# Closing stages of a streaming-encoder layer: the last expert pairs, the overflow branch and the second norm rearranged

## The chip, the cores and the metric

The kernel runs on one core of a Trainium2 chip. Times are device microseconds of that core. The kernel before takes 1161.49 us (median of 3 runs, 1161.32 to 1161.60).

## The reference

One layer, 256 tokens of 1024 values, float32. A trunk of three branches (attention, pooling, state space) ends in a first LayerNorm. Behind it stands a mixture of experts, 4 of 32 for each token, and a second LayerNorm:

```python
x = _layer_norm(DEEPNORM_ALPHA * x + mix, ln1_g[l], ln1_b[l])
ffn = _moe(x, w_router[l], b_router[l], w_up[l], b_up[l], w_down[l], b_down[l])
x = _layer_norm(DEEPNORM_ALPHA * x + ffn, ln2_g[l], ln2_b[l])
# an expert: hu = x @ w_up + b_up
#   act = min(hu_even, 7) * sigmoid(1.702 * min(hu_even, 7)) * (clip(hu_odd, -7, 7) + 1)
#   y = act @ w_down + b_down, weighted by the token's softmax gate and added to its row
```

An expert has 12 MB of weights, all 32 have 403 million bytes, and every one of them is read once.

## The kernel before, in words

*The ring.* `ring` holds 22 slots of 128 partitions x 8 KB. A weight chunk is 1 MB and fills one. `load_more` (L105) issues a transfer on SyncE for each free slot, in the order of use; `done` frees a slot behind the last product that reads it, and `release` gives it to whoever stands in `wants` (`keep`, `drop`) or back to the stream. The last two chunks come in four pieces each, alternately. The pool `con`, of constants, lies ahead of the ring in each partition; its last tile is `junk`, 4 bytes.

*Expert pairs.* The 32 experts go in `NP` = 16 pairs of 24 chunks. Each expert of a pair has 64 token slots; both share the 128 rows of the products, one on each half. `hot` makes a one-hot matrix of tokens and slots, `gather` (L958) collects the tokens' rows with it, `gates_T` (L974) makes the transposed, gate-weighted one. Then come four `up_chunk` (L1033: bias, then 8 steps of products for each expert, four chunks) and two `down_chunk` (L1041). In `products` (L1021) each chunk of work has two halves of four steps; at the start of the second half the deferred work in `pending` is issued. `swiglu`/`gate_units` (L997) is the activation: VectorE and ScalarE operations on the result of an up chunk, issued one chunk later, and two transposes back. `scatter` (L1015) adds a down chunk's result to the four accumulators `accs[t][n]` (token half t, column half n), which stay in PSUM through all pairs. The order on every engine is that of the program text (`manual_schedule`).

*The end before.* In the last pair, behind the second up chunk, five slots are taken from the ring; `row_loads` loads the four norm vectors and GpSimd broadcasts them. Behind the fourth up chunk `residual` (L1073) makes alpha * (x1 * g1 + b1) with three VectorE operations for each token half, and `add_residual` (L1080) adds it to `accs` with the identity on TensorE, in the middle of the first down chunk. Both scatters of the last pair are issued directly behind their down chunks, the first one followed by the statistics of the left columns. `overflow` (L1086) handles experts with more than 64 tokens: every engine loads the largest count into a register and branches; in these runs the branch is not entered. It stands behind the last scatter. The closing norm (L1181 to L1223) has four quarters `finish(t, n)`: (0,0) on ScalarE and GpSimd, (1,0) on TensorE with diagonal matrices, (0,1) and (1,1) on VectorE.

Of the kernel before, what the change touches and what calls it, by code (L numbers as in the profile page):

```python
# [17 lines left out]
S = 256  # L18
# [45 lines left out]
def hybrid_layer(ctx: ExitStack, tc: tile.TileContext, wt, wm, pa, pb, pc, xin, bu, lnp, b_down, out):  # L64
# [17 lines left out]
    def place(f, dt=F32):  # L82
        return ring.tile([128, 2048], dt, tag=f"w{f}", name=f"w{f}")
# [21 lines left out]
    def load_more():  # L105
        while free and state["next"] < n_chunks:
            k = state["next"]
            if k < n_chunks - 2:
                sp.dma_start(out=slot(), in_=chunk_src(k))
            elif len(free) < 2:  # L110
                break
            else:
                pair = [(slot(), chunk_src(k + i)) for i in range(2)]
                for q in range(4):
                    qs = slice(512 * q, 512 * q + 512)
                    for t, src in pair:
                        sp.dma_start(out=t[:, qs], in_=src[:, qs])

# [23 lines left out]
    ones32 = con.tile([128, 32], F32)  # L142
    epst = con.tile([128, 2], F32)
    hpi = con.tile([128, 1], F32)
    junk = con.tile([128, 1], F32)


    ph1 = ExitStack()
# [806 lines left out]

    l1 = c_("ln1")

    def gather(oh):  # L958
        xg = mw.tile([128, 8, 128], F32, tag="xg", name="xg", bufs=1)
# [12 lines left out]
        return xg  # L972

    def gates_T(oh, g):  # L974
# [4 lines left out]
        gT = mwr.tile([128, S], F32, tag="gT", name="gT")  # L979
        dve.tensor_copy(gT, pt)  # L980
        return gT

# [58 lines left out]
    def down_chunk(p, n, at):  # L1041
        py = ph.tile([128, 512], F32, tag="hu", name="py")
        products(py, N_TRUNK + 24 * p + 16 + 4 * n, at, True)
        y = mwr.tile([128, 512], F32, tag="y", name="y")
        act.activation(out=y, in_=py, func=ACTF.Copy)  # L1045
        return y

    accs = [[pacc.tile([128, 512], F32, tag=f"acc{t}{n}", name=f"acc{t}{n}") for n in range(2)] for t in range(2)]
# [15 lines left out]
    rs2 = late.tile([128, 2, 2], F32)  # L1064


    def row_loads():
        for i in range(4):
            pool.dma_start(out=row[32 * i:32 * i + 1, 0], in_=lnp[0, i:i + 1])
        for i in range(4):  # L1070
            pool.partition_broadcast(lns[i // 2][:, i % 2], row[32 * i:32 * i + 1, 0])

    def residual():  # L1073
        g, b = lns[0][:, 0], lns[0][:, 1]
        for t in range(2):
            TT(base[:, t], x1[:, t], g, op=ALU.mult)
            TT(base[:, t], base[:, t], b, op=ALU.add)
            TS(base[:, t], base[:, t], ALPHA, None, op0=ALU.mult)

    def add_residual():  # L1080
        for t in range(2):
            for n in range(2):
                pe.matmul(accs[t][n], ident, base[:, t, n * 512:(n + 1) * 512], start=False, stop=True, skip_group_check=True)


    def overflow():  # L1086
        top = nc.values_load(cmaxi, min_val=0, max_val=S)
        cnt = [0]

        def wload(e, c):  # L1090
            w = place(free[cnt[0] % 4])
            cnt[0] += 1
            sp.dma_start(out=w, in_=wm[bass.ds(e, 1), c].rearrange("o p c -> (o p) c"))
            return w.rearrange("p (k c) -> p k c", k=4)

        with tc.If(top > SLOT):
            with tc.For_i(0, NE, 1) as e:
# [5 lines left out]
                for base in range(SLOT, S, 128):  # L1103
# [6 lines left out]
                    xg, gT = gather(oh), gates_T(oh, gh)  # L1110
                    at = mw.tile([128, 8, 128], F32, tag="at", name="at")
# [8 lines left out]
                    for n in range(2):  # L1120
# [5 lines left out]
                        y = mwr.tile([128, 512], F32, tag="y", name="y")  # L1126
                        act.activation(out=y, in_=py, func=ACTF.Copy)
                        scatter(gT, y, n)
            stats(0, 0)
            stats(0, 1)  # L1130
            stats(1, 0)
            TT(z2[:, 1, 0:512], accs[1][0], lns[1][:, 0, 0:512], op=ALU.mult)

    def stats(t, n):
        dve.bn_stats(out=st2[:, t, n], in_=accs[t][n])  # L1135

    gT = None
    for p in range(NP):
        ahead = slice(2 * p + 2, 2 * p + 4)
        at = mw.tile([128, 8, 128], F32, tag="at", name="at")  # L1140
        prev = None
        for n in range(4):
            hu = up_chunk(p, n, xg)
            if (p, n) == (NP - 1, 1):

                row, base, z2, *lns = (place(free.pop(0)).rearrange("p (t d) -> p t d", t=2) for _ in range(5))
                row_loads()
            if prev is not None:
                swiglu(*prev)
            if n == 2:  # L1150
                gT = gates_T(oh, gate[:, :, 2 * p:2 * p + 2])
            if n == 3 and p + 1 < NP:
                oh = hot(val[:, :, ahead])
            prev = (hu, at, n)

        pending.append(gate_units(*prev))
        if p + 1 == NP:
            residual()
            pending.append(add_residual)
        else:  # L1160
            nxt = gather(oh)
        y = down_chunk(p, 0, at)
        if p + 1 == NP:
            act.activation(out=junk, in_=epst[:, 0:1], func=ACTF.Sqrt)
            scatter(gT, y, 0)
            stats(0, 0)
            stats(1, 0)
            TT(z2[:, 1, 0:512], accs[1][0], lns[1][:, 0, 0:512], op=ALU.mult)
        else:
            pending.append(lambda gT=gT, y=y, p=p: scatter(gT, y, 0, p == 0))  # L1170
        y = down_chunk(p, 1, at)
        if p + 1 == NP:
            scatter(gT, y, 1)
        else:
            pending.append(lambda gT=gT, y=y, p=p: scatter(gT, y, 1, p == 0))
            if p == NP // 2:
                down_bias()
            xg = nxt


    ln2 = lns[1]  # L1181
    o3 = out.rearrange("(t p) d -> t p d", p=128)
    stats(0, 1)
    pz2 = ph.tile([128, 512], F32, tag="g", name="pz2")
    overflow()
    pe.matmul(pz2, ident, ln2[:, 1, 0:512], start=True, stop=True, skip_group_check=True)
    def scale(t):
# [3 lines left out]
    def finish(t, n):  # L1191
        ns = slice(n * 512, (n + 1) * 512)
        z, acc = z2[:, t, ns], accs[t][n]
        if (t, n) == (0, 0):
            act.activation(out=z, in_=acc, func=ACTF.Identity, scale=rs2[:, t, 0:1], bias=rs2[:, t, 1:2])
            pool.tensor_tensor(z, z, ln2[:, 0, ns], op=ALU.mult)
            pool.tensor_tensor(z, z, ln2[:, 1, ns], op=ALU.add)
        elif (t, n) == (1, 0):

            sc = late.tile([128, 2, 128], F32, name="sc")  # L1200
            for i in range(2):
                TS(sc[:, i], ident, rs2[:, t, i:i + 1], None, op0=ALU.mult)  # L1202
            pe.matmul(pz2, sc[:, 0], z, start=False, stop=False, skip_group_check=True)  # L1203
            pe.matmul(pz2, sc[:, 1], ln2[:, 0, ns], start=False, stop=True, skip_group_check=True)  # L1204
            act.activation(out=z, in_=pz2, func=ACTF.Copy)  # L1205
        else:
            STT(z, acc, mv2[:, t, 0:1], ln2[:, 0, ns], op0=ALU.subtract, op1=ALU.mult)
            STT(z, z, rs2[:, t, 0:1], ln2[:, 1, ns], op0=ALU.mult, op1=ALU.add)
        if (t, n) != (0, 0):
            (act if n == 0 else sp).dma_start(out=o3[t][:, ns], in_=z)  # L1210

    for t in range(2):
        if t:
            stats(1, 1)
        dve.bn_aggr(out=mv2[:, t], in_=st2[:, t])  # L1215
        act.activation(out=rs2[:, t, 0:1], in_=mv2[:, t, 1:2], func=ACTF.Sqrt, bias=epst[:, 0:1])  # L1216
    scale(0)
    finish(0, 0)
    scale(1)
    finish(1, 0)  # L1220
    finish(0, 1)
    sp.dma_start(out=o3[0][:, 0:512], in_=z2[:, 0, 0:512])
    finish(1, 1)  # L1223
    ps3.close()


# [117 lines left out]
```

## Time and profile before

| | |
|---|---|
| median of 3 runs | 1161.49 us |
| the profiled execution, its own time | 1161.53 us |
| its span | 1159.8 us |
| busy share of the span: TensorE, VectorE, ScalarE, GpSimd | 97%, 26%, 16%, 1% |
| read from HBM | 436 MB |

The busy share of TensorE counts from the start of a matmul to its modelled end, so it does not say that the engine works at its peak. The granted clock is 1.00 nearly everywhere (mean 0.997). In the views PE is TensorE, PEld its weight loads, DVE VectorE, ACT ScalarE, POOL GpSimd, SP SyncE; a q behind an engine's name means its sequencer. A float32 product is executed in two passes, so one matmul of the program has two rows in the trace.

### The profile page before, as it was taken

The page shows a single profiled execution, that of the slowest core. Times are in us where ns is not written, and L with a number is a line of the kernel's source. Part 1 is how long each engine was busy: PE and PEld are TensorE (multiplying, and loading weights), DVE is VectorE, ACT ScalarE, POOL GpSimd, SP SyncE. Part 2 cuts the span into 40 slices and gives each one's busy share as a digit, 9 for nine tenths or more (in the row PEclk, how much of TensorE's full clock was granted, in tenths as well). Part 3 has the DMA queues.
Part 4 walks back from the last instruction along what each step waited for, and adds up shares of the span by engine and source line. Part 5 has one row for each costly group of instructions (what it writes and reads, how often), then busy time and mean ns, then how long its engine had stood idle before and what let it go on. Part 6 is the DMA issues. An engine that isn't in the chain of part 4 may idle for free. (4 is left out here: it accounts for less than half of the span.)

```text
span 1159.8 us, 13362 instructions
## 1 busy us (share of the span) xinstructions
PE 1130.4 (97%) x5535; PEld 527.4 (45%) x5535; DVE 300.9 (26%) x710; ACT 184.7 (16%) x389; POOL 13.5 (1%) x19
## 2 busy tenths in 40 slices
PE   9999999999999999999999999999999999999996
PEld 6888986643434343434343433343434344334332
DVE  4798622430202111111212121111111111111042
ACT  4555410310101010101010101010101010101002
POOL 0000000000000000000000000000000000000100
PEclk9999999999999999999999999999999999999999
DMA  9733685699999999999999999999999999999992
GB/s 368 306 110 137 243 358 212 253 423 421 420 421 421 421 421 421 421 421 420 421 422 420 421 421 420 414 422 420 422 421 420 422 420 421 421 421 420 420 412 87
DMA packets 63169, 438.05 MB, mean 378 GB/s; under 512 B 7136, under 2 KB 7648, under 8 KB 10752
## 3 DMA queue, kind: packets, MB, share of 16 engines
q1 hardware_dynamic: 62064, 435.46, 91.2%
q10 hardware_dynamic: 864, 1.54, 0.4%
q8 instruction: 45, 0.74, 0.3%
q0 software_dynamic: 176, 0.15, 0.0%
q14 instruction: 20, 0.16, 0.0%
HBM read 436.07 MB, written 1.05 MB: 377 GB/s over the span
## 5 line engine op out<-in xcount | busy, mean ns | idle before, releaser
L1028 PE MATMUL hu<-w,xg 128*64 128x512 f32 x2048 | 480.9, 596 | 14.2 <-DMA w<-in_wm_dram 14.2
L1028 PEld LDWEIGHTS hu<-w,xg 128*64 128x64 f32 x2048 | 166.0, 137 | 316.0 <-issue 262.1
L1028 PE MATMUL py<-w,at 128*64 128x512 f32 x1024 | 231.5, 597 | 0.0
L1000 DVE TENSOR_SCALAR s<-hu 128x256 f32<-128x256 f32 x64 | 27.0, 422 | 581.6 <-PE hu L1028 581.6
L1028 PEld LDWEIGHTS py<-w,at 128*64 128x64 f32 x1024 | 70.5, 136 | 136.0 <-issue 129.6
L1011 ACT ACTIVATE at<-pta 128x256 f32<-128x256 f32 x64 | 24.5, 383 | 422.9 <-PE pta L1010 422.9
L1037 PE MATMUL hu<-bup,pc_sb 128*64 128x512 f32 x256 | 68.3, 605 | 0.0
L1017 PE MATMUL acc<-y,gT 128*128 128x512 f32 x128 | 63.5, 618 | 1.5 <-ACT y L1045 1.5
L248 PE MATMUL pm<-w,w 128*128 128x256 f32 x208 | 60.6, 291 | 0.8 <-ACT vsb L641 0.8
L965 PE MATMUL pg<-oh,x 128*128 128x128 f32 x512 | 59.9, 275 | 0.0
L249 PE MATMUL pm<-w,w 128*128 128x256 f32 x208 | 58.8, 283 | 0.0
L250 PE MATMUL pm<-w,w 128*128 128x256 f32 x208 | 58.8, 282 | 0.0
L965 PEld LDWEIGHTS pg<-oh,x 128*128 128x128 f32 x512 | 58.4, 192 | 0.1
L1001 ACT ACTIVATE hu<-s 128x256 f32<-128x256 f32 x64 | 24.6, 385 | 168.3 <-DVE s L1000 168.3
L1045 ACT ACTIVATE y<-py 128x512 f32<-128x512 f32 x32 | 19.1, 597 | 190.9 <-PE py L1028 190.9
L234 DVE TENSOR_TENSOR w<-w,w 128x1024 fp32r<-128x1024 f32 x30 | 36.5, 1219 | 19.3 <-ACT w L233 19.1
L248 PEld LDWEIGHTS pm<-w,w 128*128 128x128 f32 x208 | 39.7, 191 | 3.8 <-issue 1.7
L1017 PEld LDWEIGHTS acc<-y,gT 128*128 128x128 f32 x128 | 21.7, 189 | 42.9 <-issue 39.7
L249 PEld LDWEIGHTS pm<-w,w 128*128 128x128 f32 x208 | 39.8, 191 | 0.1
L250 PEld LDWEIGHTS pm<-w,w 128*128 128x128 f32 x208 | 39.8, 191 | 0.0
L233 ACT ACTIVATE w<-w 128x1024 fp32r<-128x1024 f32 x30 | 31.6, 1057 | 35.3 <-PE pm L250 25.1
L408 PE MATMUL pm<-w,w 128*128 128x256 f32 x160 | 36.1, 383 | 1.1 <-DMA w<-in_wt_dram 1.1
(320 smaller groups left out, 681.8 us busy)
## 6 DMA issues: line engine op xcount, KB each, us to landing
w<-in_wm_dram SPq DMA_DIRECT2D x382, 1024.0 KB, 19.8
w<-in_wt_dram SPq DMA_DIRECT2D x26, 1024.0 KB, 7.9
w<-in_wm_dram SPq DMA_DIRECT2D x8, 256.0 KB, 11.7
w<-in_wt_dram SPq DMA_DIRECT2D x4, 256.0 KB, 5.6
w<-in_wt_dram ACTq DMA_DIRECT2D x4, 256.0 KB, 5.9
w<-in_wt_dram SPq DMA_DIRECT2D x2, 512.0 KB, 5.0
w<-in_xin_dram SPq DMA_DIRECT2D x1, 1024.0 KB, 7.7
w<-in_pb_dram SPq DMA_DIRECT2D x1, 896.0 KB, 8.5
```

The costliest lines, as they stand in the source:

```text
L233: act.activation(out=hi, in_=src, func=ACTF.Copy)
L234: TT(lo, src, hi.bitcast(F32), op=ALU.subtract)
L248: pe.matmul(out, whi, ahi, start=first, stop=False)
L249: pe.matmul(out, whi, alo, start=False, stop=False)
L250: pe.matmul(out, wlo, ahi, start=False, stop=last)
L408: pe.matmul(dst, w[:, k * 128:(k + 1) * 128], xt3[:, k], start=(k == 0), stop=(k == 7))
L965: pe.matmul(pg[:, b], x1[:, t, k * 128:(k + 1) * 128], oh[:, t], start=(t == 0), stop=(t == 1))
L1000: TS(xg, hu[:, 0:256], 7.0, None, op0=ALU.min)
L1001: act.activation(out=th, in_=xg, func=ACTF.Tanh, scale=0.851)
L1017: pe.matmul(accs[t][n], gT[:, t * 128:(t + 1) * 128], y, start=first, stop=True, skip_group_check=True)
L1028: pe.matmul(dst[64 * e:64 * e + 64], lhs[:, k, 64 * e:64 * e + 64], w[:, k % 4], start=first and k == 0, stop=(k == 7))
L1037: pe.matmul(hu[64 * e:64 * e + 64], ident[:, i:i + 1].to_broadcast([128, 64]), bup, start=True, stop=False)
```

## The change

The ring gets its base moved: `junk` becomes a column of a tile `scr` of 96 bytes. The last four chunks come in pieces, the first two of them in halves. Row loads and broadcasts go to pair NP-3 (the third from the end), where the four next slots released are kept; `residual` is issued there in two steps of two operations, and `add_residual` in that pair's first down chunk, behind which two slots go back. The counter is read into the registers in pair NP-4. In the last pair the activation of the second up chunk and `gates_T` are issued directly behind that chunk, then `overflow`, with weights in two free slots and its inputs in two others. The last down chunk's result is evicted in halves on ScalarE and VectorE. The left columns' scatter, statistics and products with the norm's scale are deferred into the last down chunk. The closing norm's left quarters go over TensorE (bias, diagonal matrices made by ScalarE), the right quarters and the very last step over VectorE; GpSimd has no part in it.

```diff
@@ load_more
-            if k < n_chunks - 2:
+            if k < n_chunks - 4:
                 sp.dma_start(out=slot(), in_=chunk_src(k))
             elif len(free) < 2:
                 break
             else:
                 pair = [(slot(), chunk_src(k + i)) for i in range(2)]
-                for q in range(4):
-                    qs = slice(512 * q, 512 * q + 512)
+                w = 1024 if k == n_chunks - 4 else 512
+                for q in range(0, 2048, w):
+                    qs = slice(q, q + w)
                     for t, src in pair:
                         sp.dma_start(out=t[:, qs], in_=src[:, qs])
@@ constants
-    junk = con.tile([128, 1], F32)
+    scr = con.tile([128, 24], F32)
+    junk = scr[:, 0:1]
@@ down_chunk
-        act.activation(out=y, in_=py, func=ACTF.Copy)
+        if (p, n) == (NP - 1, 1):
+            y = [y[:, 0:256], place(free[0])[:, 0:256]]
+            act.activation(out=y[0], in_=py[:, 0:256], func=ACTF.Copy)
+            dve.tensor_copy(y[1], py[:, 256:512])
+        else:
+            act.activation(out=y, in_=py, func=ACTF.Copy)
@@ residual
-    def residual():
-        g, b = lns[0][:, 0], lns[0][:, 1]
-        for t in range(2):
-            TT(base[:, t], x1[:, t], g, op=ALU.mult)
-            TT(base[:, t], base[:, t], b, op=ALU.add)
-            TS(base[:, t], base[:, t], ALPHA, None, op0=ALU.mult)
+    def residual(t):
+        base, l1r = rows_of("base"), rows_of("ln1")
+        STT(base[:, t], x1[:, t], ALPHA, l1r[:, 0], op0=ALU.mult, op1=ALU.mult)
+        STT(base[:, t], l1r[:, 1], ALPHA, base[:, t], op0=ALU.mult, op1=ALU.add)
@@ the loop over pairs
+        last = p + 1 == NP
...
+        if p == NP - 4:
+            top = nc.values_load(cmaxi, min_val=0, max_val=S)
+        if p == NP - 3:
+            for name in ("z2", "ln1", "ln2", "base"):
+                keep(name)
         for n in range(4):
             hu = up_chunk(p, n, xg)
-            if (p, n) == (NP - 1, 1):
-                row, base, z2, *lns = (place(free.pop(0)).rearrange("p (t d) -> p t d", t=2) for _ in range(5))
-                row_loads()
             if prev is not None:
                 swiglu(*prev)
-            if n == 2:
+            if p == NP - 3:
+                if n == 0:
+                    row_loads()
+                elif n > 1:
+                    residual(n - 2)
+            if n == (1 if last else 2):
                 gT = gates_T(oh, gate[:, :, 2 * p:2 * p + 2])
...
             prev = (hu, at, n)
+            if last and n == 1:
+                swiglu(*prev)
+                prev = None
+                overflow()
+                act.activation(out=junk, in_=epst[:, 0:1], func=ACTF.Tanh)
         pending.append(gate_units(*prev))
-        if p + 1 == NP:
-            residual()
+        if p == NP - 3:
             pending.append(add_residual)
...
         y = down_chunk(p, 0, at)
-        if p + 1 == NP:
+        if last:
             act.activation(out=junk, in_=epst[:, 0:1], func=ACTF.Sqrt)
-            scatter(gT, y, 0)
-            stats(0, 0)
-            stats(1, 0)
-            TT(z2[:, 1, 0:512], accs[1][0], lns[1][:, 0, 0:512], op=ALU.mult)
+            z2, ln2 = rows_of("z2"), rows_of("ln2")
+            def left_sums(y=y):
+                scatter(gT, y, 0)
+                for t in range(2):
+                    stats(t, 0)
+                    TT(z2[:, t, 0:512], accs[t][0], ln2[:, 0, 0:512], op=ALU.mult)
+            pending.append(left_sums)
...
         y = down_chunk(p, 1, at)
-        if p + 1 == NP:
-            scatter(gT, y, 1)
+        if last:
+            for t in range(2):
+                for h in range(2):
+                    pe.matmul(accs[t][1][:, h * 256:h * 256 + 256], gT[:, t * 128:(t + 1) * 128], y[h], start=False, stop=True, skip_group_check=True)
@@ closing norm (the four quarters finish(t, n) go; overflow() before them goes)
+    pz2 = [ph.tile([128, 512], F32, tag="g", name="pz2") for _ in range(2)]
+    for t in range(2):
+        pe.matmul(pz2[t], ident, ln2[:, 1, 0:512], start=True, stop=False, skip_group_check=True)
+    sc = late.tile([128, 2, 2, 128], F32, name="sc")
+    def moments(t):
+        stats(t, 1)
+        dve.bn_aggr(out=mv2[:, t], in_=st2[:, t])
+        act.activation(out=rs2[:, t, 0:1], in_=mv2[:, t, 1:2], func=ACTF.Sqrt, bias=epst[:, 0:1])
+    def scales(t):
         dve.reciprocal(rs2[:, t, 0:1], rs2[:, t, 0:1])
         STT(rs2[:, t, 1:2], mv2[:, t, 0:1], -1.0, rs2[:, t, 0:1], op0=ALU.mult, op1=ALU.mult)
+        for i in (1, 0) if t == 0 else (1,):
+            act.activation(out=sc[:, t, i], in_=ident, func=ACTF.Copy, scale=rs2[:, t, i:i + 1])
+    def left(t):
+        z = z2[:, t, 0:512]
+        pe.matmul(pz2[t], sc[:, t, 1], ln2[:, 0, 0:512], start=False, stop=(t == 1), skip_group_check=True)
+        if t == 0:
+            pe.matmul(pz2[t], sc[:, t, 0], z, start=False, stop=True, skip_group_check=True)
+            act.activation(out=z, in_=pz2[t], func=ACTF.Copy)
+            act.dma_start(out=o3[t][:, 0:512], in_=z)
+    def right(t):
+        z = z2[:, t, 512:1024]
+        STT(z, accs[t][1], mv2[:, t, 0:1], ln2[:, 0, 512:1024], op0=ALU.subtract, op1=ALU.mult)
+        STT(z, z, rs2[:, t, 0:1], ln2[:, 1, 512:1024], op0=ALU.mult, op1=ALU.add)
+        sp.dma_start(out=o3[t][:, 512:1024], in_=z)
+    moments(0)
+    moments(1)
+    scales(0)
+    scales(1)
+    left(0)
+    left(1)
+    right(0)
+    right(1)
+    z = z2[:, 1, 0:512]
+    STT(z, z, rs2[:, 1, 0:1], pz2[1], op0=ALU.mult, op1=ALU.add)
+    sp.dma_start(out=o3[1][:, 0:512], in_=z)
```

## Rows read from the trace of the kernel before

**Rows 1.** The page: its span, and GB/s in 40 slices of 29 us.

```profile
span 1159.8 us, 13362 instructions
...
GB/s 368 306 110 137 243 358 212 253 423 421 420 421 421 421 421 421 421 421 420 421 422 420 421 421 420 414 422 420 422 421 420 422 420 421 421 421 420 420 412 87
```

**Rows 2.** A window, stream's end: us, busy (count) of PE..POOL, clock, DMA share, GB/s.

```profile
1136.00:1137.00 1.00, 1.00 (x3) 0.38 (x2) 0.20 (x1) 0.99 (x2) 0.00 (x0) 1.00 0.25 92
```

**Rows 3.** Timeline of SyncE, last weight transfers: start us, us, line, operation, tile.

```profile
1129.35 0.33 SPq L117 DMA_DIRECT2D w<-in_wm_dram  x1
...
1131.82 0.33 SPq L117 DMA_DIRECT2D w<-in_wm_dram  x1
```

**Rows 4.** Timeline, last pair: start, us, line, operation, tiles, count [idle before <-releaser].

```profile
1097.18 3.65 PE L1028 MATMUL hu<-w,xg 128*64 128x512 f32 x14 [0.84 <-DMA w<-in_wm_dram]
...
1100.76 0.44 PE L1010 MATMUL pta<-pc_sb,s 128*128 128x128 f32 x2
...
1101.13 1.08 PE L1037 MATMUL hu<-bup,pc_sb 128*64 128x512 f32 x4
...
1126.26 1.98 PE L1083 MATMUL acc<-w,pc_sb 128*128 128x512 f32 x4 [0.34 <-DVE w L1078]
...
1129.38 1.98 PE L1083 MATMUL acc<-w,pc_sb 128*128 128x512 f32 x4 [1.14 <-DVE w L1078]
...
1137.56 7.09 PE L1028 MATMUL py<-w,at 128*64 128x512 f32 x32
...
1145.43 1.98 PE L1017 MATMUL acc<-y,gT 128*128 128x512 f32 x4 [0.78 <-ACT y L1045]
...
1149.94 1.10 PE L1186 MATMUL pz<-w,pc_sb 128*128 128x512 f32 x2 [2.53 <-PEq L1096]
...
1155.82 0.36 ACTq L1210 DMA_DIRECT2D out_dram<-w  x1
```

**Rows 5.** Groups by line, last 75 us: count | busy, mean ns | idle.

```profile
L1135 DVE BATCH_NORM_STATS2 st<-acc 128x6 f32<-128x512 f32 x4 | 2.8, 699 | 16.8 <-PE acc L1017 15.3 <-PEq L1096 1.5
...
L1207 DVE SCALAR_TENSOR_TENSOR w<-acc,mv,w 128x512 f32<-128x512 f32 x2 | 1.5, 742 | 0.0
...
L1045 ACT ACTIVATE y<-py 128x512 f32<-128x512 f32 x2 | 1.2, 597 | 16.3 <-PE py L1028 16.3
...
L980 DVE COPY gT<-ptw 128x256 f32<-128x256 f32 x1 | 0.4, 424 | 6.8 <-PE ptw L978 6.8
...
L1215 DVE BATCH_NORM_AGGREGATE mv<-st 128x2 f32<-128x12 f32 x2 | 0.4, 209 | 0.7 <-DVEq L1096 0.6
...
L1168 DVE TENSOR_TENSOR w<-acc,w 128x512 f32<-128x512 f32 x1 | 0.7, 674 | 0.0
```

**Rows 6.** The branch's line, on TensorE's sequencer: count, ns min/median/max, start us.

```profile
L1096 PEldq COMPARE_BRANCH  x1: 3489/3489/3489, 1146.0 to 1146.0; - x1
```

**Rows 7.** Windows of the tail, columns as in rows 2.

```profile
1151.00:1152.00 1.00, 0.46 (x2) 0.30 (x2) 0.97 (x5) 0.64 (x1) 0.00 (x0) 0.91 0.00 0
...
1152.00:1153.00 1.00, 1.00 (x2) 0.34 (x1) 0.89 (x2) 0.00 (x0) 0.87 (x1) 0.50 0.03 8
...
1155.00:1156.00 1.00, 0.15 (x1) 0.00 (x0) 0.61 (x1) 0.60 (x1) 0.06 (x1) 0.88 0.56 211
```

**Rows 8.** DMA queues: 400:600, 1153:1159.8 and 1136.9:1137.5 us; packets, MB, share of 16 engines.

```profile
q1 hardware_dynamic: 11542, 84.05, 101.1%
...
q1 hardware_dynamic: 432, 0.79, 31.0%
...
q14 instruction: 1, 0.01, 3.2%
```

**Rows 9.** DMA issues on the page: tiles, engine, count, KB each, us to landing.

```profile
w<-in_wm_dram SPq DMA_DIRECT2D x382, 1024.0 KB, 19.8
...
out_dram<-w SPq DMA_DIRECT2D x3, 256.0 KB, 2.1
...
out_dram<-w ACTq DMA_DIRECT2D x1, 256.0 KB, 2.7
```

More of the change, by code (lines that the diff above doesn't have):

```diff
@@ L956, in hybrid_layer, with gather @@
     l1 = c_("ln1")
-    def gather(oh):
-        xg = mw.tile([128, 8, 128], F32, tag="xg", name="xg", bufs=1)
+    def gather(oh, xg=None):
+        if xg is None:
+            xg = mw.tile([128, 8, 128], F32, tag="xg", name="xg", bufs=1)
         for g in range(2):
@@ L972, in gather, with gates_T @@
         return xg
-    def gates_T(oh, g):
+    def gates_T(oh, g, gT=None):
         TT(oh, oh, g[:, :, :, None].to_broadcast([128, 2, 2, SLOT]), op=ALU.mult)
@@ L978, in gates_T @@
             pe.transpose(pt[:, t * 128:(t + 1) * 128], oh[:, t], ident)
-        gT = mwr.tile([128, S], F32, tag="gT", name="gT")
+        if gT is None:
+            gT = mwr.tile([128, S], F32, tag="gT", name="gT")
         dve.tensor_copy(gT, pt)
@@ L1064, in hybrid_layer, with rows_of @@
     rs2 = late.tile([128, 2, 2], F32)
+    def rows_of(name):
+        return big[name][0].rearrange("p (t d) -> p t d", t=2)
     def row_loads():
+        row = rows_of("z2")
         for i in range(4):
@@ L1070, in row_loads @@
         for i in range(4):
-            pool.partition_broadcast(lns[i // 2][:, i % 2], row[32 * i:32 * i + 1, 0])
-    def residual():
-        g, b = lns[0][:, 0], lns[0][:, 1]
-        for t in range(2):
-            TT(base[:, t], x1[:, t], g, op=ALU.mult)
-            TT(base[:, t], base[:, t], b, op=ALU.add)
-            TS(base[:, t], base[:, t], ALPHA, None, op0=ALU.mult)
+            pool.partition_broadcast(rows_of(f"ln{i // 2 + 1}")[:, i % 2], row[32 * i:32 * i + 1, 0])
+    def residual(t):
+        base, l1r = rows_of("base"), rows_of("ln1")
+        STT(base[:, t], x1[:, t], ALPHA, l1r[:, 0], op0=ALU.mult, op1=ALU.mult)
+        STT(base[:, t], l1r[:, 1], ALPHA, base[:, t], op0=ALU.mult, op1=ALU.add)
     def add_residual():
+        base = rows_of("base")
         for t in range(2):
@@ L1083, in add_residual @@
                 pe.matmul(accs[t][n], ident, base[:, t, n * 512:(n + 1) * 512], start=False, stop=True, skip_group_check=True)
+        drop("base")
+        drop("ln1")
     def overflow():
-        top = nc.values_load(cmaxi, min_val=0, max_val=S)
+        assert state["next"] == n_chunks
         cnt = [0]
+        oxa = place(free[2]).rearrange("p (a k c) -> p a k c", a=2, k=8)
+        ogT = place(free[3])[:, 0:S]
         def wload(e, c):
-            w = place(free[cnt[0] % 4])
+            w = place(free[cnt[0] % 2])
             cnt[0] += 1
@@ L1109, in overflow @@
                     oh = hot(vh)
-                    xg, gT = gather(oh), gates_T(oh, gh)
-                    at = mw.tile([128, 8, 128], F32, tag="at", name="at")
+                    xg, gT, at = gather(oh, oxa[:, 0]), gates_T(oh, gh, ogT), oxa[:, 1]
                     for n in range(4):
@@ L1141, in hybrid_layer @@
         prev = None
+        if p == NP - 4:
[3 more added lines that the diff above has]
+                keep(name)
         for n in range(4):
             hu = up_chunk(p, n, xg)
-            if (p, n) == (NP - 1, 1):
-                row, base, z2, *lns = (place(free.pop(0)).rearrange("p (t d) -> p t d", t=2) for _ in range(5))
-                row_loads()
             if prev is not None:
                 swiglu(*prev)
-            if n == 2:
+            if p == NP - 3:
[4 more added lines that the diff above has]
+            if n == (1 if last else 2):
                 gT = gates_T(oh, gate[:, :, 2 * p:2 * p + 2])
-            if n == 3 and p + 1 < NP:
+            if n == 3 and not last:
                 oh = hot(val[:, :, ahead])
             prev = (hu, at, n)
+            if last and n == 1:
[3 more added lines that the diff above has]
+                act.activation(out=junk, in_=epst[:, 0:1], func=ACTF.Tanh)
         pending.append(gate_units(*prev))
-        if p + 1 == NP:
-            residual()
+        if p == NP - 3:
             pending.append(add_residual)
-        else:
+        if not last:
             nxt = gather(oh)
         y = down_chunk(p, 0, at)
-        if p + 1 == NP:
+        if last:
             act.activation(out=junk, in_=epst[:, 0:1], func=ACTF.Sqrt)
-            scatter(gT, y, 0)
-            stats(0, 0)
-            stats(1, 0)
-            TT(z2[:, 1, 0:512], accs[1][0], lns[1][:, 0, 0:512], op=ALU.mult)
+            z2, ln2 = rows_of("z2"), rows_of("ln2")
[5 more added lines that the diff above has]
+            pending.append(left_sums)
         else:
@@ L1178, in hybrid_layer @@
             xg = nxt
-    ln2 = lns[1]
     o3 = out.rearrange("(t p) d -> t p d", p=128)
[L1183 to L1187, printed above, removed]
+    pz2 = [ph.tile([128, 512], F32, tag="g", name="pz2") for _ in range(2)]
+    for t in range(2):
+        pe.matmul(pz2[t], ident, ln2[:, 1, 0:512], start=True, stop=False, skip_group_check=True)
+    sc = late.tile([128, 2, 2, 128], F32, name="sc")
@@ L1188, in scale @@
+    def moments(t):
[3 more added lines that the diff above has]
+    def scales(t):
         dve.reciprocal(rs2[:, t, 0:1], rs2[:, t, 0:1])
         STT(rs2[:, t, 1:2], mv2[:, t, 0:1], -1.0, rs2[:, t, 0:1], op0=ALU.mult, op1=ALU.mult)
[L1191 to L1223, printed above, removed]
+        for i in (1, 0) if t == 0 else (1,):
+            act.activation(out=sc[:, t, i], in_=ident, func=ACTF.Copy, scale=rs2[:, t, i:i + 1])
```

1 line of the change is left out of this document (removed).

## The prediction

> **What bounds the kernel now.** I read the slices of the span first, then windows of the middle and of the end, then SyncE's queue in order of time, then TensorE's timeline of the last expert pair. [rows 1] From about 230 us on the transfers run flat at 421 GB/s with the DMA engines busy all the time; TensorE is busy too, but it has slack, since each half of a chunk begins with a wait for a weight transfer (0.84 us before 1097.18 [rows 4]; the other halves of the pair are of this kind). So the weight stream sets the pace up to its last byte, and nothing before that is worth anything unless it makes a transfer faster. SyncE issues one transfer per landing, every 2.48 us [rows 3], the last at 1131.82; bytes move until about 1137 [rows 2]. The span ends at 1159.8. These 23 us behind the stream are what the change can reach, and in them two things are seen [rows 4]: TensorE stops for the residual (1126.26 to 1131.36, 1.14 us of it waiting for VectorE), so that the whole last down chunk starts only at 1137.56, when all its weights are there, and ends at 1144.65; then 15.15 us follow to the end (scatter, overflow branch, norm, stores).
>
> **The sum, made against the profiled run** (span 1159.8, time 1161.53, so 1.73 lie around the span; the median of the runs is 1161.49, practically the same).
>
> *Residual and row loads two pairs earlier.* Off the last pair go 8 passes of the identity (two groups of 1.98 us [rows 4]) and the wait between them, 5.1 us in all. In pair NP-3 the same 8 passes and four vector operations come back, now two per half of the rows instead of three. There TensorE has the slack seen above, some 1 us in each 10 us, and this pair and the next are 120 us long: I cost it at 0; without that cover it would be 3.9 us. Broadcasts on GpSimd and the row loads move along; the vector work behind them waits one chunk, and TensorE first needs VectorE's result a chunk later still. Four ring slots of 22 are held for one pair, then two: SyncE has 8 transfers out at a time (19.8 us from issue to landing at 2.48 us each) and its issue waits for a landing, not for a slot, so 0; if a slot were late, 2.48 us each.
>
> *The last four chunks in pieces.* The stream's end stays: the old last chunks in pieces of 256 KB kept the pace of 2.48 us per MB (1131.82 to about 1137 is 2 MB). TensorE may begin the first quarter of the last down chunk some 2.5 us before its half has landed. 0 by itself, bounds -0.5 and +0.5.
>
> *The overflow branch amid the last pair.* It leaves the tail, where TensorE idled 2.53 us for it (the wait before 1149.94 [rows 4]). On TensorE the branch itself took 3489 ns, on the other engines 45 to 72 ns [rows 6]. (The Trainium skill, "Runtime: NRT & Kernel Launch", Instruction fetch mechanics, says that a taken branch out of the fetched window has to fetch its target by DMA first; the row agrees. It speaks against the new place, where such a fetch meets the weight stream.) Behind the branch on TensorE now wait 2 up and 2 down chunks, and they are followed by everything else. Its arrival: the second up chunk ends where it does now, 1100.8; two pairs of transposes of some 0.35 us; then, because the second chunk's activation is no longer put behind the third chunk, TensorE waits for a chain of VectorE copy, four operations and ScalarE's tanh beside one of them, five of 0.42 us [rows 5] with gaps, 2.2 us; transposes again, 1104.1; the branch from 1103.75, 3.49, and 0.4 to the first load: 1107.65. What is queued: third and fourth up chunk, each 0.9 of bias (1.08 [rows 4] with some 0.2 of drain) and 7.0 (two halves, 3.58 from one to the next instruction), 15.8; first down chunk 7.16 and two transposes, 0.8; last down chunk 3.58, scatter of its neighbour 1.9, then 3.65: 32.9 in sum, 1140.55. All weights are there in time (the half of 1126.9 is awaited by nothing, the last quarters land by 1137). Two things are added. The engine has stood for 2.2 and 3.5 us; in the tail of before, after standing for 2.53 us, its granted clock fell to 0.50, the 1.2 GHz level, at about 1151.8 and was back at 1155.2 (means of 0.91, 0.50 and 0.88 [rows 7]), 3.4 us; I take one such stretch, in which 1.7 us of work is lost: **1142.2**. And the branch under load: bounds 0 (it hides nothing there) and 19.8 us (a fetch that stands behind the stream like a weight load); I take 0 extra, since the row of the branch itself is the nearest. The best case is set by the stream: the half landed at 1131.82 leaves 1.75, 1.9 and 3.65: 1139.2. The counter that the branch tests is now read in pair NP-4, by every engine: on SyncE behind seven transfers that are already out, on TensorE in the waits for weights, below 2.5 us (all that the read and the branch cost in the tail), so 0; the gate transposes move one chunk up and find their inputs ready, 0. ScalarE's table load behind the branch falls in the free time of two chunks. SyncE reaches the branch only after its last issue, waits there for all landings until about 1137.6, and holds up the output stores alone, which come later.
>
> *The tail, counted from TensorE's last down product T (now T is 1144.65, the tail 15.15).* Eviction in halves on ScalarE and VectorE, 0.13 and 0.42 [rows 5] instead of 0.13 and 0.60; scatter from T+0.6 in half-width pieces, same columns, 1.98 [rows 4], its first half done at T+1.6. Statistics 0.70, aggregate 0.21, twice, to T+3.5 on VectorE; the square root of the first lies beside them, that of the second ends at 3.9, and reciprocal and product of both at 4.2. TensorE meanwhile puts the bias into both banks, 4 passes of 0.43, which keep it going until 4.2; then ScalarE's diagonal matrices (128 columns each, below the 0.60 of 512 [rows 5]) and six passes, 2.6 us, to T+7.0. VectorE: four operations of 0.74 and 0.67 [rows 5] for the right halves, to T+7.1, and the last one, 0.74, which takes the bank just finished: T+7.9. Its store takes 2.1 us [rows 9] and the end of the span 1.3 more (before, ScalarE's store issued at 1155.82 [rows 4] lands 2.7 later [rows 9], at 1158.5), with 0.2 for the issue: **T+11.5**. So 15.15 becomes 11.5, of which 2.5 is the branch. If the clock is at the lower level there, six passes take twice the 2.6 us, and some more: T+14.2. The lower end is T+10.8.
>
> Span 1142.2 + 11.5 = 1153.7, time **1155.4**: 6.1 us below, 2.4 of it before T and 3.7 behind.
>
> *The ring at 1 KB multiples.* 64 bytes more ahead of it; before, every slot began 192 bytes past a multiple of 256. What a packet costs [rows 8]: the stream's packets took 101.1% of 16 engines for 200 us; 84.05 MB are 10260 of 8 KB, 315 ns each. The stores' 2 KB packets took 87.8 ns (31.0% of 16 x 6.8 us over the 384 that 0.79 MB are). So 8 KB cost 301 ns of bytes and some 14 of a fixed part, 4.4%. The gain lies between 0 and all of it over the 905 us of the flat stream, 40 us. I take 0: a packet of 8 KB of the instruction queue, which has nothing to do with the ring, takes 307 ns on an empty fabric (3.2% of 16 x 0.6 us), so the fixed part is there without the ring's offset.
>
> **The rivals.**
> 1. *Alignment counts.* If a packet that begins off a 256-byte line touches 33 lines instead of 32, each is 3.0% shorter afterwards: 905 us x 3.0% = 27 us, time **1128**. TensorE could follow (it waits in every half). For it: the fixed part is large enough. Against: the instruction packet. (The rule is that of the Trainium skill, "DMA: Bandwidth & Descriptors", How a descriptor splits into AXI transactions: a descriptor off a 256-byte boundary costs an extra transaction. No run here has an aligned ring, so nothing shows it yet.) Chance 0.14.
> 2. *The branch waits for the stream (slower).* Place: TensorE at 1103.75. Price: anything up to 19.8 us instead of 3.5. It decides from 9.6 us on, where the 6.1 us are gone; with the full price T is near 1158.5, the time **1172**. For it: the fetch goes through the same 16 engines. Against: instruction packets are fetched all through the stream, and TensorE shows no such gap [rows 4]. Chance 0.08.
> 3. *The gain is eaten (no change).* The branch costs 3 us more and the clock is low again in the tail: T 1145.2, tail 14.2, time **1161**; what is saved in one place is paid in another. Chance 0.09.
>
> **How the numbers follow.** Forecast 0.69: 1155.4, its own range 1151.7 (T 1139.2, tail 10.8) to 1159.3. The range to hold 8 in 10 reaches from 1146, which takes in a small effect of the alignment, to 1161; outside are rival 1 in full and rival 2. Within 0.2% is 2.3 us, about what this kernel's measurement can tell from no change. Faster 0.69 + 0.14 = 0.83, same 0.09, slower 0.08.
>
> **What would show it.** In the changed profile: transfers still at 421 GB/s in the middle (425 and more: rival 1); TensorE idle for 3.5 to 5 us around 1104 to 1108 at the branch (over 9: rival 2), and a clock of 0.50 soon after; the last down products ending near 1142 without waits for DMA but those of the pieces; no branch behind the scatter; the last store issued 8 us after T by SyncE, released by VectorE. I am wrong if the end of the stream itself moves, or if T is that of before.

## The result, and the profile after

| | before | after |
|---|---|---|
| median, runs side by side (4 each) | 1161.55 us | 1147.38 us |
| ratio | | 0.9877 (0.9860 to 0.9894) |
| profiled execution: time, span | 1161.53, 1159.8 | 1147.84, 1146.1 |
| last weight bytes | 1136.6 | 1126.3 |
| end of the last down product, T | 1144.65 | 1134.38 |
| T to the end of the span | 15.15 | 11.72 |

The change gains 14.2 us where 6.1 were forecast. In the span of the profiled runs 10.3 of 13.7 us are the stream's earlier end; T lies as far behind it as before, 8.0 us; and 3.4 are the tail's.

Six of the runs told of below, of kernels with slots at a multiple of 256 bytes, took 6 to 18 us more than their fellows; that is taken up behind the offsets.

The page of the changed kernel, against [rows 1]:

```profile
span 1146.1 us, 13388 instructions
...
GB/s 358 325 90 132 243 358 248 222 415 427 427 426 426 426 427 427 427 426 427 426 427 426 428 426 427 420 428 426 426 427 426 427 426 427 426 426 427 427 416 117
```

The flat stretch is at 427 GB/s, not 421. The row of its queue from 400 to 600 us (packets, MB, share of 16 engines), against [rows 8]:

```profile
q1 hardware_dynamic: 11693, 85.17, 100.9%
```

More bytes came in the same 200 us, with the engines as busy. In the records of the single packets the mean time of one of 8 KB between 300 and 1100 us went from 314.3 to 309.6 ns: before, 7% of them took 309 and nearly all others 311 to 321; after, 99.7% took 309. So the floor of 309 stayed, and what went is the spread above it.

TensorE's timeline in the last pair, against [rows 4]:

```profile
1089.32 0.44 PE L1015 MATMUL pta<-pc_sb,s 128*128 128x128 f32 x2
1089.59 0.38 PE L982 MATMUL ptw<-pc_sb,oh 128*128 128x128 f32 x2
1092.77 0.41 PE L1015 MATMUL pta<-pc_sb,s 128*128 128x128 f32 x2 [2.79 <-DVE s L1010]
1099.08 1.98 PE L1042 MATMUL hu<-bup,pc_sb 128*64 128x512 f32 x4 [5.90 <-PEq L1114]
...
1110.50 7.05 PE L1033 MATMUL hu<-w,xg 128*64 128x512 f32 x32
...
1121.80 7.09 PE L1033 MATMUL py<-w,at 128*64 128x512 f32 x32
1128.82 1.98 PE L1022 MATMUL acc<-y,gT 128*128 128x512 f32 x4
1130.73 3.65 PE L1033 MATMUL py<-w,at 128*64 128x512 f32 x16
```

The two waits are the chain of the activation (2.79) and the branch (5.90). Behind them no product waits for a weight: TensorE works off its lateness to the end. The branch's row on its sequencer, against [rows 6]:

```profile
L1114 PEldq COMPARE_BRANCH  x1: 5972/5972/5972, 1092.8 to 1092.8; - x1
```

Windows around it (busy time and count of PE, PEld, DVE, ACT and POOL, granted clock, DMA share, GB/s):

```profile
1094.00:1096.00 2.00, 0.00 (x0) 0.00 (x0) 0.00 (x0) 0.00 (x0) 0.00 (x0) 0.63 1.04 438
1096.00:1104.00 8.00, 4.92 (x12) 1.65 (x14) 0.00 (x0) 0.00 (x0) 0.00 (x0) 0.50 1.01 421
1104.00:1105.00 1.00, 1.00 (x6) 0.34 (x4) 0.00 (x0) 0.00 (x0) 0.00 (x0) 0.62 0.95 401
1105.00:1110.00 5.00, 5.00 (x26) 1.80 (x24) 0.07 (x1) 0.00 (x0) 0.00 (x0) 1.00 1.01 427
```

From 1094.5 to 1104.8 the clock is at its lower level of 1.2 GHz (0.50), 5.7 us of that under work. The end of the chain of waits (start, us, engine, tile, line):

```profile
1134.52 0.39 ACT y L1053
1134.91 0.04 issue
1134.96 1.17 PE acc L1206 x4
1136.13 0.02 issue
1136.15 0.71 DVE st L1148
...
1140.83 0.75 DVE w L1243
1141.58 0.72 DVE w L1255
```

It runs as forecast: eviction, scatter, statistics, and VectorE to T+7.9. There is no branch in it.

### The profile page after: what moved, and what is told of

It reads as the page before. It is cut to its first block, busy times and chain, and to the rows that moved or that the text cites. A ratio compares the mean times of both kernels' runs of the same rounds, so it can differ in the third digit from the quotient of the medians.

```text
span 1146.1 us, 13388 instructions
## 1 busy us (share of the span) xinstructions
PE 1121.5 (98%) x5543; PEld 518.7 (45%) x5543; DVE 298.9 (26%) x709; ACT 183.8 (16%) x391; POOL 10.5 (1%) x17
## 5 line engine op out<-in xcount | busy, mean ns | idle before, releaser
L1033 PE MATMUL hu<-w,xg 128*64 128x512 f32 x2048 | 472.4, 598 | 5.7 <-DMA w<-in_wm_dram 5.7
L1033 PEld LDWEIGHTS hu<-w,xg 128*64 128x64 f32 x2048 | 155.8, 138 | 310.4 <-issue 284.8
L1015 PEld LDWEIGHTS pta<-pc_sb,s 128*128 128x128 f32 x128 | 12.8, 140 | 54.1 <-issue 54.1
```

The source lines that it names most:

```text
L1033: pe.matmul(dst[64 * e:64 * e + 64], lhs[:, k, 64 * e:64 * e + 64], w[:, k % 4], start=first and k == 0, stop=(k == 7))
```

## The experiments

**Where do 12 us come from?** Theory A: from the ring's offset alone. C: from the other edits, or from where the other tiles lie.

The ring alone, on the kernel before, and its counterpart, everything but the ring:

```diff
-    junk = con.tile([128, 1], F32)
+    scr = con.tile([128, 24], F32)
+    junk = scr[:, 0:1]
```
```diff
-    scr = con.tile([128, 24], F32)
+    scr = con.tile([128, 1], F32)
```

> The kernel before with one edit: the tile ahead of the ring is 96 bytes instead of 4, so that every ring slot begins at a multiple of 1 KB. Theory A (the ring's offset sets the packet time): the middle of the stream goes from 421 to 427 GB/s, its 8 KB packets from a mix of 309 to 319 ns to 309 alone, the last weight lands about 11 us earlier, the tail stays at 15.15 us, and the time is 1150.5 us (1149.5 to 1151.5). Theory C (the gain comes from the other edits, or was this one build's luck): 421 GB/s and 1161.5 us.

> The changed kernel with the 4-byte tile ahead of the ring, so that the slots begin 192 bytes past a multiple of 256 as before; everything else of the change stays. Theory A: 421 GB/s, the last weight lands near 1137, and what is left of the gain is that of the tail less what the branch costs: 1158.4 us (1157.5 to 1159.5). Theory C: 427 GB/s and 1147.4 us.

Measured beside 1161.79 us of before: the ring alone 1149.35 us, ratio 0.9891 (0.9875 to 0.9908); all but the ring 1159.76, 0.9981 (0.9971 to 0.9990). The window from 400 to 500 us, the ring alone and all but the ring:

```profile
400.00:500.00 100.00, 100.00 (x477) 37.84 (x474) 16.98 (x42) 11.40 (x27) 0.00 (x0) 1.00 1.01 427
```
```profile
400.00:500.00 100.00, 100.00 (x478) 37.83 (x475) 16.97 (x42) 11.39 (x27) 0.00 (x0) 1.00 1.01 421
```

The rate goes with the ring, and the times add up: 12.4 us by the ring put in, 12.4 by the ring taken out (1159.76 - 1147.38), and 2.0 for all the rest. C falls. Both times lie a little outside A's ranges: the ring gave 1.2 us more than A put (1150.5), the rest 1.4 less (1158.4).

The 64 bytes move every tile behind the ring too. With a pad behind the ring these stay at their old offset from a multiple of 256 bytes:

```diff
+    pad_pool = ctx.enter_context(tc.tile_pool(name="padp", bufs=1))
+    pad = pad_pool.tile([128, 48], F32)
```

> The kernel before with the ring at a multiple of 1 KB and 192 bytes put behind it, so that the tiles behind the ring stay at 192 past a multiple of 256 as before. Theory A (the ring alone matters, since what is written by the stream is the ring): 427 GB/s, 1149.4 us (1148.8 to 1150.2). Theory C' (the other tiles' places matter): 421 GB/s, or 427 with a time above 1151.

1149.37 us, ratio 0.9894 (0.9877 to 0.9910), 427 GB/s. So it is the ring's own place that counts.

**Which multiple?** The kernel before with other widths of `scr`, 40, 56, 16, 88, 152 and 216 in place of 24:

> The kernel before with 160 bytes ahead of the ring: slots 64 bytes past a multiple of 256. Theory A: as before, 421 GB/s and 1161.5 us. Theory G with a unit of 64 bytes: 427 GB/s; with a unit of 128: 421 GB/s.

> The kernel before with 224 bytes ahead of the ring: slots 128 bytes past a multiple of 256. Theory A: 421 GB/s and 1161.5 us. Theory G (64 or 128 bytes are the unit, and 192 past 256 is slow only for its part of 64): 427 GB/s and 1149.4 us.

> The kernel before with 64 bytes ahead of the ring where it had 32: slots 224 bytes past a multiple of 256, that is, 32 past a multiple of 64. Theory A (aligned or not is all that counts): 421 GB/s and 1161.5 us. Theory H (each finer misalignment costs more): below 421 GB/s, 1165 us or more.

> The kernel before with 352 bytes ahead of the ring: its slots begin 256 bytes past a multiple of 1 KB. Theory A (a multiple of 256 bytes is enough): 427 GB/s in the middle, packets of 309 ns, about 1149.4 us. Theory B (1 KB or 512 bytes are needed): 421 GB/s, 312 to 320 ns among the packets, about 1161.5 us.

> The kernel with slots 256 bytes past a multiple of 1 KB once more, timed in rounds: its first run had 426 to 427 GB/s everywhere but in one stretch from 722 to 787 us at 388 GB/s (packets of 342 to 345 ns), which no other run has. Theory A (the stretch was a disturbance from outside, a multiple of 256 is enough): no such stretch, 1149.4 us. Theory B' (the offset from 1 KB brings such stretches): the stretch comes back, 1155 us.

> The kernel before with 608 bytes ahead of the ring: slots 512 bytes past a multiple of 1 KB. Theory A (a multiple of 256 bytes is enough): 427 GB/s, 1149.4 us, all runs within 1 us. Theory B' (places off a multiple of 1 KB bring slower stretches into some runs): a median of 1149.4 us with some runs of 1155 to 1161 us.

> The kernel before with 864 bytes ahead of the ring: slots 768 bytes past a multiple of 1 KB. Theory A: 427 GB/s, 1149.4 us, all runs within 1 us. Theory B': some runs of 1155 to 1161 us. If 512 is clean and 768 is not, a multiple of 512 is the unit.

> The kernel before with slots at a multiple of 1 KB, once more, on the same chip as the two others. Both theories: 1149.4 us, all runs within 1 us. Longer runs here too would say that they come from outside and not from the offset.

| slots begin at | GB/s, 400 to 500 us | time, us |
|---|---|---|
| 64 past 256 | 421 | 1161.58, one run |
| 128 past 256 | 421 | 1161.24, one run |
| 192 past 256 (before) | 421 | 1161.4 to 1161.8 |
| 224 past 256 | 420 | 1164.56, one run |
| 256 past 1 KB | 427 | 1155.48, one run; again: 1149.39, 8 runs to 1160.79 |
| 512 past 1 KB | 427 | 1149.38, 4 runs to 1149.86 |
| 768 past 1 KB | 427 | 1149.45, 5 runs to 1158.6 |
| 1 KB | 427 | 1149.62, 6 runs to 1167.25 |

The window from 400 to 500 us at 128 past 256, and at 256 past 1 KB (the first of its runs):

```profile
400.00:500.00 100.00, 100.00 (x477) 37.79 (x474) 16.96 (x42) 11.39 (x27) 0.00 (x0) 1.00 1.01 421
```
```profile
400.00:500.00 100.00, 100.00 (x477) 37.81 (x474) 16.96 (x42) 11.39 (x27) 0.00 (x0) 1.00 1.01 427
```

A multiple of 256 bytes is enough. Each of 64, 128 and 192 past one costs the same 1.5% (314 ns a packet), and 224 past, which is 32 off a multiple of 64, a little more, in theory H's direction (315.3 ns, 1164.6 us in its one run). G falls with the rows for 64 and 128, B with those for 256 and 768. That one of the three offsets is as dear as the other fits a step per packet, not one per byte. (The Trainium skill, "DMA: Bandwidth & Descriptors", How a descriptor splits into AXI transactions, has both: a descriptor off a 256-byte boundary has one transaction more, and the bytes fetched in vain cost beats. As an estimate from that page, by the first an 8 KB packet would have 33 for 32, 3.1%, at any offset; by the second the price would rise with the offset. From 64 to 192 the runs agree with the first in form and not in size.)

The longer runs don't follow the offset: they are there at 1 KB too, which theory B' does not allow; and theory A's "all runs within 1 us" fell too. Two of them were profiled, and show one stretch that is slower than the rest. Here 768 past 1 KB, GpSimd's timeline, then windows:

```profile
715.12 0.83 POOL L1054 DMA_DIRECT2D bdn<-in_b_down_dram  x1 [499.16 <-DMA w<-in_wm_dram]
```
```profile
722.00:787.00 65.00, 63.95 (x274) 23.04 (x274) 9.32 (x23) 5.89 (x14) 0.00 (x0) 0.97 1.01 387
787.00:822.00 35.00, 30.52 (x130) 10.72 (x127) 6.45 (x16) 1.82 (x5) 0.00 (x0) 1.00 1.01 387
830.00:890.00 60.00, 58.87 (x266) 23.12 (x264) 9.32 (x23) 5.89 (x14) 0.00 (x0) 1.00 1.01 427
```

100 us at 387 for 427 GB/s are 9.4 us, about what this run took more (1158.6 for 1149.45). In the other (1155.48) the stretch goes from 722 to 787. Both begin some 7 us behind the issue of GpSimd's load of the down biases, in these kernels the one load of another engine in the middle of the stream; every profiled run has a brief dip there (5 us at 368 to 409 GB/s), and only some don't come out of it at once. That the load is the cause is not shown, and no run was without it. None of the runs at 421 GB/s was so long.

**What does the branch cost in its new place?** Theory D: the branch with its wait and the low clock behind it make TensorE late for the end of the stream. E: it would have been late anyway.

```diff
                 swiglu(*prev)
                 prev = None
-                overflow()
-                act.activation(out=junk, in_=epst[:, 0:1], func=ACTF.Tanh)
```

> The changed kernel without the overflow branch (the handling of experts with more than 64 tokens is left out; in these data it is not entered). Theory D (the branch with its wait and the low clock behind it makes TensorE late for the end of the stream): the clock stays at 1.00 through the last pair, the last down product ends about 3 us behind the last weight instead of 8.4 us, and the time is 1142 us (1141 to 1143.5). Rival E (TensorE would have been late anyway, the stream's last pieces or the deferred work set it): 1146.5 to 1147.5 us.

1141.13 us, ratio 0.9821 (0.9805 to 0.9837), 6.2 us below the changed kernel. T is 1128.09, 2.8 us behind the stream's end (1125.32). D's time holds, its clock did not: behind the 2.80 us wait that is left TensorE still has 3.4 us at 0.50. The wait in TensorE's timeline, then windows:

```profile
1093.11 0.41 PE L1015 MATMUL pta<-pc_sb,s 128*128 128x128 f32 x2 [2.80 <-DVE s L1010]
```
```profile
1090.00:1094.00 4.00, 1.20 (x7) 0.50 (x7) 2.03 (x5) 1.16 (x3) 0.00 (x0) 0.95 1.01 426
1094.00:1097.00 3.00, 3.00 (x10) 0.89 (x8) 0.00 (x0) 0.00 (x0) 0.00 (x0) 0.50 1.01 426
```

The branch kept, but entered without the wait (the branch's body, with the PSUM tag "g" in it, leaves the chunk's result alone):

```diff
             if last and n == 1:
-                swiglu(*prev)
-                prev = None
                 overflow()
@@ overflow, both products
-                        hu = ph.tile([128, 512], F32, tag="hu", name="hu")
+                        hu = ph.tile([128, 512], F32, tag="g", name="hu")
```

> The changed kernel with the second up chunk's activation again put behind the third up chunk, so that TensorE enters the branch without the 2.8 us wait for VectorE and ScalarE (the branch's body, not entered, uses the other PSUM buffers). Theory D: the wait of 2.8 us goes; the branch itself still takes 3.5 to 6 us; the clock still falls for a stretch: 1144.5 us (1143.5 to 1146). Rival F (the branch is served with the fetch that it starts when TensorE arrives, and the low clock follows from the whole stand, so a shorter stand of 5.9 us keeps the clock up): 1142.5 us. Rival E: 1147.4 us, no change.

**1142.65 us**, ratio 0.9835 (0.9819 to 0.9852): the fastest of all with nothing left out, 4.7 us below the changed one. TensorE's timeline and the branch's row:

```profile
1085.86 3.65 PE L1033 MATMUL hu<-w,xg 128*64 128x512 f32 x14 [0.26 <-DMA w<-in_wm_dram]
1089.43 0.44 PE L1015 MATMUL pta<-pc_sb,s 128*128 128x128 f32 x2
1089.71 0.38 PE L982 MATMUL ptw<-pc_sb,oh 128*128 128x128 f32 x2
1091.90 1.08 PE L1042 MATMUL hu<-bup,pc_sb 128*64 128x512 f32 x4 [1.82 <-PEq L1114]
...
1125.58 3.65 PE L1033 MATMUL py<-w,at 128*64 128x512 f32 x16
```
```profile
L1114 PEldq COMPARE_BRANCH  x1: 5792/5792/5792, 1085.9 to 1085.9; - x1
```

The branch takes about as long as in the changed kernel, 5.79 us, but it begins at 1085.9, while TensorE works off a half of an up chunk and the transposes that are queued already. 4 us lie beside that work, and 1.82 are left. In the changed kernel a wait stood ahead of it, so that the sequencer came to the branch with nothing queued but two transposes (0.41 us). The clock stays at 1.00:

```profile
1094.00:1097.00 3.00, 3.00 (x14) 0.97 (x10) 0.00 (x0) 0.00 (x0) 0.00 (x0) 1.00 1.03 423
```

F had the time and the clock right, for another reason than it gave: TensorE stands idle for 1.82 us, not 5.9.

The branch back at the end, behind the last scatter, and the second up chunk's activation behind the third, the rest as changed (the left columns' statistics, made earlier, are made again in the branch's body, which is not entered):

```diff
@@ overflow, the end of its body
+            for t in range(2):
+                stats(t, 0)
+                TT(z2[:, t, 0:512], accs[t][0], ln2[:, 0, 0:512], op=ALU.mult)
@@ the loop over pairs
             if last and n == 1:
-                swiglu(*prev)
-                prev = None
-                overflow()
-                act.activation(out=junk, in_=epst[:, 0:1], func=ACTF.Tanh)
+                pass
@@ closing norm
+    overflow()
     for t in range(2):
         pe.matmul(pz2[t], ident, ln2[:, 1, 0:512], start=True, stop=False, skip_group_check=True)
```

> The changed kernel with the overflow branch put back behind the last scatter, and the second up chunk's activation behind the third. Theory D (moving the branch into the last pair cost more than it saved, since it opened with a wait and closed with a low clock): TensorE follows the stream and ends its last down product near 1128.2; behind it the branch costs 2.5 us of standing and a stretch at the low clock some 1.7: 1145.5 us (1144.3 to 1146.8), below the changed kernel's 1147.4. Rival E' (in the tail the branch costs what it saved, with a low clock through the closing norm): 1147.4 us or more.

1144.73 us, ratio 0.9855 (0.9839 to 0.9872): the move of the branch, as it was made, cost 2.65 us. Its rows for the tail, from TensorE's timeline:

```profile
1124.03 3.65 PE L1033 MATMUL py<-w,at 128*64 128x512 f32 x16
...
1133.12 1.96 PE L1219 MATMUL pz<-w,pc_sb 128*128 128x512 f32 x4 [2.84 <-PEq L1114]
```

T is 1127.68, and 15.12 follow to the end of its span (1142.8), as many as before: with the branch there, the new norm saves nothing. (The old norm without the branch was not run.)

The pieces, on the kernel without the wait, where TensorE is not late:

```diff
-            if k < n_chunks - 4:
+            if k < n_chunks - 2:
...
-                w = 1024 if k == n_chunks - 4 else 512
+                w = 512
```

> The kernel of the branch without the wait (1142.65 us), with only the last two chunks in pieces, four each, as before. Theory D: TensorE is only a microsecond behind the stream there, so that a half that lands later could be felt, but the bytes and their order are nearly the same: within 0.5 us of 1142.65. Rival I (the pieces let TensorE start the last chunks earlier): 1144 us or more.

1144.45 us, ratio 0.9851 (0.9834 to 0.9867): 1.8 us more, rival I. Its timeline has a wait that the other has not:

```profile
1115.88 4.63 PE L1033 MATMUL py<-w,at 128*64 128x512 f32 x18
1121.81 3.65 PE L1033 MATMUL py<-w,at 128*64 128x512 f32 x14 [1.30 <-DMA w<-in_wm_dram]
```

A half is 16 rows. So the 18 are the second half of the first down chunk and the first step of the last one, for the one expert; the other expert's weights for it come as a whole chunk of 1 MB, which lands at 1121.77. In the kernel that it is compared with, the first piece of these weights landed at 1119.09, and the half ran through.

## Why the prediction was right in sign and wrong in size

*The ring at 1 KB multiples, "I take 0".* This is the step that failed, a term put at nothing that is worth 12.4 us, more than all else together. The reason given was that an instruction packet of 8 KB, which has nothing to do with the ring, takes 307 ns [rows 8], so the fixed part does not come from the offset. That holds for the larger part of it, and it answers another question. The same packet said that 307 was to be had, and the stream's mean was 315: the difference, 2.5%, stood in the two rows, and the fixed part had been weighed as a whole, all or nothing. (Its size was off too: 315 less 87.8 ns for 6 KB more makes 303 ns of bytes and 12 fixed, not 301 and 14.) What the offset cost is 4.7 ns of these 12. The chance of 0.14 went to rival 1, which had the cause, an offset from 256 bytes, at twice its size: 3.0% for 1.5%. Its sign in the profile, "425 and more", came, and so did the forecast's own sign of being wrong, that "the end of the stream itself moves". That the time still lies in the range that was to hold 8 in 10, from 1146, is luck: with the ring's 12.4 us and all else as forecast it would have been 1143.0; what the other edits fell short by, 4.1 us, brought it back.

*The branch amid the last pair.* Forecast from the end of the second up chunk (1100.76) to T: 41.4 us. Measured from 1089.3 (the transposes behind the same chunk begin there): 45.1. Of the 3.7 us, 2.9 lie ahead of the first weights that TensorE loads after the branch (6.9 forecast, 9.8 measured). Behind it the clock, for which one stretch of 3.4 us was put, from the tail's [rows 7], was low for 10.2, and took 2.8 us of work for 1.7; the queued work itself was some 0.4 shorter than put. No table load of ScalarE stands behind the branch, as the forecast had it; the only one in the last pair is at 1126.12, for the square root. The wait ahead of the branch was seen (2.2, measured 2.79), but not what it does: without it the branch lies beside queued work (1.82 us left of 5.79). The price of the branch itself was taken from a quiet tail, 3.49; under the stream it is 5.97 and 5.79. So for "the branch under load", "I take 0 extra" was short by 2.5 us, far from the bound of 19.8. (The Trainium skill, "Runtime: NRT & Kernel Launch", Instruction fetch mechanics, says a taken branch may have to fetch its target by DMA. The traces agree.) Inside the branch's time there is one 16 KB packet of an instruction queue, q8, in either place: it begins 1.0 us behind the branch's start in the tail of before, 3.6 us in the stream, and the branch ends 1.4 to 1.5 us behind it. So the packet begins 2.6 us later under the stream, about the time of one chunk. The row of that queue before, from 1147 to 1148.1 us, and in the changed kernel, from 1096.3 to 1097.4 us:

```profile
q8 instruction: 1, 0.02, 5.7%
```
```profile
q8 instruction: 1, 0.02, 5.3%
```

*T behind the stream.* 5.2 us were forecast (1142.2 and "about 1137"), 8.0 came, the same as before, so that nothing of what the residual and the pieces saved was seen in T. With the branch out of the way they show: 2.8 us in three kernels (without the branch, without the wait, with the branch late).

*The residual and the row loads, 0 in their new place.* Right as far as it can be told: the kernel with the branch late ends its stream 0.4 us behind that of the ring alone. Taken alone, the residual was not tried.

*The pieces, 0 with bounds of 0.5.* Too small; 1.8 us where TensorE follows the stream. The forecast named the place, the last down chunk begun "some 2.5 us before its half has landed", and gave it no price; the wait that goes there is 1.30 us. In the changed kernel, where TensorE is late and waits for no weight, the pieces were not tried alone.

*SyncE waits for landings, not for slots.* Right, but with the branch in the stream a landing comes late. In the changed kernel one issue of SyncE waited 3.5 us for a landing; without a branch the longest is 2.1, with the branch late 2.2. In all four profiled kernels with the branch in the stream one landing of the last pair comes 3.9 to 4.0 us behind the one before, some 11 to 12 us after the branch began, where a chunk takes 2.4 to 2.5; without the branch there, none. The changed kernel, from 1080 to 1110 us (line, what for: us in total, times, longest):

```profile
SPq L109 <- DMA w<-in_wm_dram: 14.4, 7, 2.1
SPq L118 <- DMA w<-in_wm_dram: 11.9, 5, 3.5
```

The stream ends 1.0 to 1.4 us later for it (1126.33 against 1125.32 without a branch and 1124.88 with the branch late). How the branch holds up a landing was not tested.

*The tail from T, 11.5.* 11.72 measured, and 11.4 to 11.9 in all kernels with the branch in the pair or out. But the parts were wrong: by the kernel with the branch late the branch is the whole 3.4 us, not 2.5, and the new norm gives nothing beside it (15.12 us; other profiled kernels with the old norm and the branch have 14.6 to 15.4).

*Rivals 2 and 3.* The branch did not wait for the stream as rival 2 had it (9.6 us and more). Rival 3 came half true for the other edits: some 3 us more for the branch, though the tail kept its clock; 2.0 us were left of the 6.1, and with the ring's old offset the kernel is 0.19% faster. The two errors have opposite signs: 12.4 missed, 4.1 given too much.

## What to carry to other kernels

Compare the records of equal packets, not only the rate: where a stream's packets spread above a floor that some of them reach, ask where their destination begins, before asking for anything else. A buffer that takes a whole stream belongs on a multiple of 256 bytes in its partition; 64 bytes of padding were worth 1.07% here. And put a branch where its engine's queue is full: here taking the wait away, with the branch kept, gained 4.7 us, and leaving the branch out, with the wait kept, 6.2.

## What the runs showed of the hardware that was not expected

- An 8 KB packet takes 309 ns into a slot at a multiple of 256 bytes, and 314.2 to 314.3 on average at 64, 128 or 192 past one, 315.3 at 224 past: a mix of 309, 311 to 315 and 318 to 321, with the same floor.
- TensorE's branch took 3.39 to 3.90 us in the tail of twelve profiled kernels and 5.79 to 5.99 us amid the weight stream of four, and its sequencer can begin it 4 us ahead of the end of the products queued before.
- How long TensorE stood idle does not tell whether its clock falls. A stand of 2.80 us in the pair was followed by 3.4 us at 0.50, and one of 2.84 us in the tail of another kernel by none, with the clock at 1.00 to the norm's end; 1.82 us were followed by none either. The old tail, with stands of 2.43 to 2.87 us, was profiled eleven times: ten times the clock fell to 0.50 behind it, and once, behind 2.70 us, not (slots 256 past 1 KB, the second time).
- Two profiled runs at 427 GB/s fell to 387 GB/s for 65 and 100 us, from 7 us behind a load on GpSimd's queue; it stays open what starts it and what ends it.
